# Down products of a two-layer trunk by seven products instead of eight, with the combined down weights summed in DRAM

## The chip, the cores and the metric

The kernel runs on one core of a Trainium2 chip. The metric is the device time of the whole program in microseconds (us), the median of several executions, lower is better. TensorE (PE) multiplies, VectorE (DVE) and ScalarE (ACT) work elementwise, GpSimd (POOL) does small odd jobs, and SyncE (SP) issues the loads. All engines run their own instruction lists and meet at semaphores. Sixteen DMA engines move data between DRAM and the on-chip memory.

## The reference, cut to what matters

512 tokens of width 1024 in float32 go through two layers. In layer 0 the mixer is differential attention beside a gated short convolution, in layer 1 it is a spatial gating unit. Around the mixer and around the feed-forward part stand RMS norms. The feed-forward part of each layer `i`, which the change touches, is

```python
h = rms_norm(x, norm_g[i, 2])
f = (jax.nn.silu(h @ w_gate[i]) * (h @ w_up[i])) @ w_down[i]
x = x + rms_norm(f, norm_g[i, 3])
```

`w_gate` and `w_up` are 1024 x 2816, `w_down` is 2816 x 1024. The last product of that line is called the down product here, and the 512 x 2816 matrix that it takes from the left the hidden matrix.

## The kernel before, in words

**Numbers.** Each float32 operand of a matmul is split into a rounded part `hi` and a rest `lo` (`split`, L136 on ACT and L137 on DVE), and each product is three matmuls: hi by hi, lo by hi, hi by lo (`PASSES`). Splitting 128x1024 elements takes one cast on ACT and one subtraction on DVE.

**Stages.** First come layer 0's projections and attention. Then, in each layer: the output projection of the mixer (`out_proj`), the feed-forward products of gate and up (`ffn`, L550), the down product (`out_proj` again, L110), and the norms between them. Gate and up are computed already by Strassen's scheme: seven products of half-size blocks stand for eight, with combined weights that DVE sums (L215) and combined tokens (`Combined`). The hidden matrix goes to `pair_` tiles, one for each of the 11 units of 256 hidden columns.

**The down product before.** `ffn` ends with `out_proj(Hidden(hidden), 5, ...)`. Eight PSUM banks hold four token tiles by two column halves. For each of the 22 blocks of 128 hidden columns, three matmuls of 128x512 go into each bank: 22 x 8 x 3 = 528 matmuls in each layer. The weights come as 11 chunks of 1 MB and are split in 22 pieces; `Hidden` splits the hidden matrix in 11. The last five blocks are held back, so that the four token tiles end one after the other and `post_norm` of one runs beside the matmuls of the next.

**Order.** `order` and `take` fix the order in which weight chunks are loaded and split, and three `raw` buffers let the loads run ahead. `Clock` counts modelled PE time: `clock.after(wait, step)` writes a step into the program later, `clock.beat` moves the time with each matmul. A scheduler of the framework then lays out each engine's list: among the instructions whose inputs it believes ready it takes the one written first, so an instruction that is written late but has no inputs to wait for can move far ahead on an engine that it believes idle.

**POOL before.** POOL's list is short. In the attention it has one multiplication for each block (`combine`, L732; 4 heads by 4 blocks), whose result DVE adds (L735) and PE transposes (L743), and one power for each norm (`power`, L301). Four pre-norms at the start use the same line. No DMA is issued by POOL; all loads and stores go through SP.

```python
            nc.gpsimd.tensor_scalar(out=probs[1][:, 0:w], in0=probs[1][:, 0:w],
                                    scalar1=c1[:, 0:1], scalar2=None, op0=ALU.mult)
            clock.after(TO_TURN // 2, lambda: turn(at))
```

Of the kernel before, what the change touches and what calls it, by code (L numbers as in the profile page):

```python
# [18 lines left out]
P = 128  # L19
# [6 lines left out]
NF = FFN // P  # L26
RMS_EPS = 1e-6
# [17 lines left out]
class Clock:  # L45
# [4 lines left out]
    def __init__(self):  # L50
        self.now, self.n, self.queue = 0.0, 0, []

# [19 lines left out]
def trunk(  # L72
# [36 lines left out]
    def mm(out, lhsT, rhs, start, stop):  # L109
        nc.tensor.matmul(out, lhsT, rhs, start=start, stop=stop)  # L110
        clock.beat(max(230.0 * rhs.shape[-1] / 512, 108.0))
# [48 lines left out]
    def plan_rows(w, ks):  # L160

        for k in ks[::2]:
            c = Chunk([P, 2, D], [(ALL, w[k * P:(k + 2) * P, :].rearrange("(k p) f -> p k f", p=P))])
            for m in range(2):
                plan(None, c, (ALL, slice(m, m + 1), ALL))

# [61 lines left out]

    FIRST, THEN, STEADY = (7, 3), (1, 2, 4, 6, 5), (1, 2, 4, 6, 5, 7, 3)

    def plan_ffn(layer):
        units = [Unit(layer, c * 256) for c in range(FFN // 256)]
# [10 lines left out]
        plan_rows(w_down[layer], range(NF))  # L243
# [168 lines left out]

    def mean_square(parts):

        ms, a = small(2), small(1)
# [3 lines left out]
        nc.vector.scalar_tensor_tensor(out=a[:, 0:1], in0=ms[:, 0:1], scalar=ms[:, 1:2],  # L419
                                       in1=eps_t, op0=ALU.add, op1=ALU.add)  # L420
        return power(a[:, 0:1], 1), a
# [26 lines left out]
    def post_norm(t, halves, g, wait, then, store):  # L448

        f = row_tile()  # L450
        y0, a = mean_square(halves)
        for n, c in enumerate(HALVES):
            nc.vector.tensor_tensor(out=f[:, c], in0=halves[n], in1=g[:, c], op=ALU.mult)  # L453

        def add():
            y = newton(y0, a[:, 0:1], 1)
            for c in HALVES:
                nc.vector.scalar_tensor_tensor(out=xs[t][:, c], in0=f[:, c], scalar=y,  # L458
                                               in1=xs[t][:, c], op0=ALU.mult, op1=ALU.add)
                if store:  # L460
                    nc.sync.dma_start(out=out[0, t * P:(t + 1) * P, c], in_=xs[t][:, c])
            if then:
                then(t)

        clock.after(wait, add)
# [18 lines left out]
    def out_proj(lhs, n_held, g_post, then, next_ahead, wait=2000, store=False):  # L484
# [13 lines left out]
        for k in range(first):  # L498
            w2 = take(min(2 + k, n_held, n_k - 1 - k))
            lhs.ahead(k + 2)  # L500
# [5 lines left out]
        lhs.ahead(n_k)  # L506
        ahead(n_held)
        held = [take(0) for k in range(n_held)]
        for t in range(NT):
# [3 lines left out]
            post_norm(t, acc[t], g_post, wait, then, store)  # L513
# [3 lines left out]
    class Mixed:  # L517
# [5 lines left out]
        def ahead(self, n):  # L523
            pass

# [3 lines left out]
    class Hidden:  # L529


        def __init__(self, tiles):
            self.tiles, self.n, self.parts = tiles, 2 * len(tiles), []

        def ahead(self, n):
            while 2 * len(self.parts) < min(n, self.n):
                self.parts.append(split(self.tiles[len(self.parts)]))

        def at(self, k, part):
            return self.parts[k // 2][part][:, k % 2, :]  # L540
# [14 lines left out]
    FIRST_TOKENS, LAST_TOKENS = slice(0, 256), slice(256, 512)  # L555

    def ffn(layer, units, hT, g_post, then, next_ahead, store=False):
        hidden = []
# [11 lines left out]
        def finish(c, f, cols, pair_):  # L570

            nc.scalar.activation(out=c[:, 0:256], in_=c[:, 0:256], func=AF.Silu)  # L572
            nc.vector.tensor_tensor(out=pair_[:, f, cols], in0=c[:, 0:256], in1=c[:, 256:512],
# [13 lines left out]
        for i, u in enumerate(units):  # L587
            pair_ = act([P, 2, 512])
            hidden.append(pair_)
# [4 lines left out]
            finish(plus(y, a), 0, LAST_TOKENS, pair_)  # L594
            if i < EARLY:
# [4 lines left out]
                finish(plus(r, u2), 1, LAST_TOKENS, pair_)  # L600
                run(x, u, 5, False)
                v = copied(x)
                finish(plus(z, v), 0, FIRST_TOKENS, pair_)
                finish(plus(x, p7), 1, FIRST_TOKENS, pair_)
# [388 lines left out]
```

## Time and profile before

| what | value |
|---|---|
| median of 3 runs | 1097.82 us (1097.77 to 1098.58) |
| profiled execution, its own time | 1097.55 us |
| its span in the profile | 1095.8 us |
| PE / weight loads / DVE / ACT / POOL busy | 97% / 87% / 66% / 45% / 4% |
| moved by DMA | 111.33 MB, 102 GB/s over the span |

The profile shows one execution. Busy shares are averages over stages that differ; a matmul's own duration overlaps with that of its neighbours, so the pace of PE is read from how many matmuls a stretch of the chain holds. "PEclk" is the clock granted to TensorE as a share of full speed; full speed is the higher of its two levels, 2.4 GHz, and half of it the lower, 1.2 GHz. POOL's instructions stand in the timeline in the order of POOL's list.

### The profile page before, as it was taken

To read this page: it belongs to the slowest core of one execution; us is meant where nothing else is said; L and a number is where in the kernel's file an instruction comes from. 1 tells how busy PE (TensorE), PEld (TensorE's weight loads), DVE (VectorE), ACT (ScalarE), POOL (GpSimd) and SP (SyncE) were. 2 spreads that over 40 slices of the span, in tenths; PEclk is the share of its full clock that TensorE was granted. 3 is DMA by queue.
4 is the path that set the end of the run, shared out by engine and by line. 5 is a ranking of instruction groups with operands and counts; after the bars stand their busy time and mean duration, and the time that the engine had idled before them with its cause. 6 is when DMAs were issued, how large, how long until landed. Compare 5 with 4: busy or idle time off the path is not lost.

```text
span 1095.8 us, 15882 instructions
## 1 busy us (share of the span) xinstructions
PE 1065.2 (97%) x6527; PEld 952.4 (87%) x6527; DVE 728.5 (66%) x1083; ACT 496.8 (45%) x831; POOL 45.2 (4%) x67
## 2 busy tenths in 40 slices
PE   8999999988999999999999999988999999999997
PEld 6777778878999999988888888878999999988886
DVE  4566665598887887873328454779888787883304
ACT  4466444256544454553315333345554454573201
POOL 0011210010000000000001000010000000000000
PEclk8999999998999999999999999998999999999999
DMA  8321222313333233254202231411333323362002
GB/s 314 105 72 59 94 77 79 114 39 118 114 115 116 78 117 116 99 214 149 85 31 78 77 124 69 154 38 59 116 116 108 124 78 115 115 224 87 1 1 77
DMA packets 77770, 111.33 MB, mean 102 GB/s; under 512 B 2769, under 2 KB 63326, under 8 KB 77698
## 3 DMA queue, kind: packets, MB, share of 16 engines
q1 hardware_dynamic: 77698, 110.33, 30.2%
q8 instruction: 51, 0.84, 0.3%
q14 instruction: 21, 0.17, 0.1%
HBM read 108.21 MB, written 2.11 MB: 101 GB/s over the span
## 4 chain that ended last, share of the span: by engine, by line
PE 86%; DVE 8%; ACT 2%; issue 1%; POOL 1%; DMA 1%; SPq 0%; POOLq 0%; DVEq 0%; ACTq 0%
PE ps L110 44%; PE ps L550 38%; DVE wlo L137 1%; DVE hTlo L383 1%; POOL s L301 1%; DVE h L431 1%; ACT j L417 1%; DVE x L458 1%; PE ps L441 1%; PE ps L751 1%; DVE t L388 1%; DMA raw<-in_w_in_even_dram 1%; PE ps L937 1%; DVE wsum L215 1%; ACT whi L136 1%
## 5 line engine op out<-in xcount | busy, mean ns | idle before, releaser
L550 PE MATMUL ps<-hThi,whi 128*128 128x256 f32 x1232 | 276.3, 287 | 7.8 <-ACT hThi L382 7.3
L550 PE MATMUL ps<-hThi,wlo 128*128 128x256 f32 x1232 | 276.7, 285 | 0.0
L550 PE MATMUL ps<-hTlo,whi 128*128 128x256 f32 x1232 | 274.3, 285 | 0.0
L137 DVE TENSOR_TENSOR wlo<-raw,whi 128x1024 fp32r<-128x1024 f32 x166 | 199.0, 1223 | 65.2 <-ACT whi L136 34.4
L550 PEld LDWEIGHTS ps<-hThi,whi 128*128 128x128 f32 x1232 | 205.6, 195 | 10.1 <-ACT hThi L382 8.6
L550 PEld LDWEIGHTS ps<-hThi,wlo 128*128 128x128 f32 x1232 | 206.4, 194 | 0.1
L550 PEld LDWEIGHTS ps<-hTlo,whi 128*128 128x128 f32 x1232 | 204.9, 194 | 0.4 <-DVE hTlo L383 0.4
L136 ACT CAST whi<-raw 128x1024 fp32r<-128x1024 f32 x166 | 169.2, 1047 | 55.0 <-PE ps L110 37.4
L110 PE MATMUL ps<-whi,wlo 128*128 128x512 f32 x352 | 137.1, 390 | 0.0
L110 PE MATMUL ps<-wlo,whi 128*128 128x512 f32 x352 | 137.0, 389 | 0.0
L110 PE MATMUL ps<-whi,whi 128*128 128x512 f32 x352 | 136.7, 389 | 0.0
L137 DVE TENSOR_TENSOR wlo<-wsum,whi 128x1024 fp32r<-128x1024 f32 x88 | 105.8, 1221 | 29.5 <-ACT whi L136 25.7
L136 ACT CAST whi<-wsum 128x1024 fp32r<-128x1024 f32 x88 | 90.1, 1043 | 71.1 <-DVE wsum L215 53.6
L110 PE MATMUL ps<-whi,a 128*128 128x512 f32 x256 | 80.0, 391 | 0.0
L110 PEld LDWEIGHTS ps<-whi,whi 128*128 128x128 f32 x352 | 66.1, 188 | 13.7
L110 PEld LDWEIGHTS ps<-wlo,whi 128*128 128x128 f32 x352 | 66.1, 188 | 13.6
L110 PEld LDWEIGHTS ps<-whi,wlo 128*128 128x128 f32 x352 | 66.1, 188 | 13.5
L572 ACT ACTIVATE t<-t 128x256 f32<-128x256 f32 x88 | 36.1, 417 | 86.0 <-DVE t L562 85.8
L562 DVE TENSOR_TENSOR t<-ps,t 128x512 f32<-128x512 f32 x88 | 58.5, 686 | 15.1 <-PE ps L550 14.4
L567 ACT COPY t<-ps 128x512 f32<-128x512 f32 x70 | 40.8, 583 | 61.2 <-PE ps L550 61.0
L301 POOL TENSOR_TENSOR s<-s,neg_half 128x1 f32<-128x1 f32 (+1 forms) x40 | 25.4, 634 | 960.3 <-DVE s L419 887.2
L453 DVE TENSOR_TENSOR h<-ps,g 128x512 f32<-128x512 f32 x32 | 21.7, 685 | 63.0 <-ACT j L417 63.0
(131 smaller groups left out, 1325.4 us busy)
## 6 DMA issues: line engine op xcount, KB each, us to landing
raw<-in_w_gate_dram SPq DMA_DIRECT2D x44, 512.0 KB, 3.8
raw<-in_w_up_dram SPq DMA_DIRECT2D x44, 512.0 KB, 4.7
raw<-in_w_down_dram SPq DMA_DIRECT2D x22, 1024.0 KB, 4.8
raw<-in_w_in_even_dram SPq DMA_DIRECT2D x10, 1024.0 KB, 5.5
raw<-in_w_in_odd_dram SPq DMA_DIRECT2D x8, 1024.0 KB, 5.1
g<-in_norm_g_dram SPq DMA_DIRECT2D x8, 512.0 KB, 3.7
raw<-in_w_out_even_dram SPq DMA_DIRECT2D x4, 1024.0 KB, 4.8
raw<-in_w_out_odd_dram SPq DMA_DIRECT2D x4, 1024.0 KB, 5.0
```

The source lines that it names most:

```text
L110: nc.tensor.matmul(out, lhsT, rhs, start=start, stop=stop)
L136: nc.scalar.copy(out=hi, in_=src)
L137: nc.vector.tensor_tensor(out=lo, in0=src, in1=hi.bitcast(F32), op=ALU.subtract)
L215: nc.vector.tensor_tensor(out=t, in0=x, in1=y, op=op)
L301: nc.gpsimd.tensor_tensor(out=y0[:, :n], in0=a, in1=neg_half[:, :n], op=ALU.pow)
L383: nc.vector.tensor_tensor(out=lo, in0=src, in1=hi.bitcast(F32), op=ALU.subtract)
L388: minus = lambda out, x, y: nc.vector.tensor_tensor(out=out, in0=x, in1=y, op=ALU.subtract)
L453: nc.vector.tensor_tensor(out=f[:, c], in0=halves[n], in1=g[:, c], op=ALU.mult)
L550: nc.tensor.matmul(bank[:, m * 256:(m + 1) * 256], piece[a][:, m, k, :], hT.at(b, p)[:, k, :], start=first and m == 0 and i == 0, stop=i = ...
L562: nc.vector.tensor_tensor(out=c, in0=x, in1=y, op=ALU.add)
L567: nc.scalar.copy(out=c, in_=x)
L572: nc.scalar.activation(out=c[:, 0:256], in_=c[:, 0:256], func=AF.Silu)
```

## The change

The 2816 rows of the down weights are taken as 11 units of two blocks (j = 0, 1), the 1024 columns as two halves, the 512 tokens as two halves. Seven products of 256 tokens x 1408 x 512 columns replace the eight: 7 products x 11 units x 2 token tiles x 3 = 462 matmuls in each layer. Four of the seven right-hand sides are sums of two, three or four quarters of the down weights.

- `Down.sums` makes these sums in DRAM: four tensors `t` (named `tsum` in the rows) for each layer, each in three groups of 4, 4 and 3 units. A group is copied from one quarter (`ALU.bypass`) and then another quarter or sum is added to it (`ALU.add`), both as DMAs issued by POOL from DRAM to DRAM. That is 24 copies and 24 adds for two layers, up to 1 MB each. `t[2]` needs `t[1]` finished, `t[4]` needs `t[2]` finished.
- These DMAs are handed to `clock.slow`, from which `beat` takes one per 7000 ns of modelled time: layer 0's from the attention on, layer 1's from layer 0's third feed-forward unit on.
- `Down.plan` loads seven quarters or sums per layer through SP, in pieces of at most two units of 512 columns (42 splits for each layer, where there were 22).
- `Hidden` now keeps 12 raw tiles, sums them on DVE in place (`differ`, `piece`: 12 instructions for each layer) and splits 21 pieces (where there were 11).
- `down_proj` runs the products in the order 1, 2, 6, 5, 3, 7, 4 in three pairs of PSUM banks and combines them by ACT copies and DVE additions (`copied`, `plus`). `PostNorm` is the norm after the products with its squares split by column half. The first two token tiles end after the fifth product, the last two after the seventh, of which seven units are held back.
- POOL's space for DMA descriptors grows from 1024 to 4096.

```diff
@@ class Clock
+        self.slow, self.next_slow = [], 0.0
     def beat(self, ns):
         self.now += ns
+        if self.slow and self.now >= self.next_slow:
+            self.next_slow = self.now + 7000
+            self.slow.pop(0)()
@@ trunk
+    class Down:
+        ORDER = (1, 2, 6, 5, 3, 7, 4)
+        GROUPS = (slice(0, 4), slice(4, 8), slice(8, UNITS))
...
+        def sums(self):
+            q, t = self.q, self.t
+            copies = ((t[1], q[0, 0]), (t[3], q[0, 1]), (t[2], q[1, 1]), (t[4], q[1, 0]))
+            adds = ((t[1], q[0, 1]), (t[3], q[1, 1]), (t[2], t[1]), (t[4], t[2]))
+            return [lambda to=to, of=of, g=g, op=op: nc.gpsimd.dma_start(
+                        out=to[:, g, :], in_=of[:, g, :], accum_op=op)
+                    for g in self.GROUPS
+                    for op, pairs in ((ALU.bypass, copies), (ALU.add, adds)) for to, of in pairs]
...
     class Hidden:
+        def differ(self, g):
+            r = self.raw
+            n = act(list(r[0, 0, g].shape))
+            r["n", g] = n
+            nc.vector.tensor_tensor(out=n, in0=r[1, 1, g], in1=r[0, 1, g], op=ALU.subtract)
+            nc.vector.tensor_tensor(out=r[0, 1, g], in0=r[0, 0, g], in1=r[0, 1, g],
+                                    op=ALU.subtract)
...
+    def down_proj(down, lhs, g_post, then, next_ahead, store, wait=2000):
+        n_held = 7
...
+        run(x, 1, last=False)
+        c11 = [copied(x[t]) for t in both]
+        run(y, 2)
...
+        run(x, 6, first=False, last=False)
+        c12 = [copied(x[t]) for t in both]
+        run(q, 5, last=False)
+        c22 = [copied(q[t]) for t in both]
+        run(q, 3, first=False)
+        for t in both:
+            norms[t].close([(1, plus(q[t], c12[t]), -1)])
+        run(x, 7, first=False, last=False)
...
+        finish = run(x, 4, first=False, held=n_held)
+        for t in both:
+            finish(t)
+            norms[t].close([(0, x[t], 1)])
+            ahead(next_ahead[t])
@@ ffn
+            if i == EARLY and layer == 0:
+                clock.slow += downs[1].sums()
...
-        lhs = Hidden(hidden)
-        lhs.ahead(4)
-        out_proj(lhs, 5, g_post, then, next_ahead, store=store)
+        down_proj(downs[layer], hidden, g_post, then, next_ahead, store)
@@ attention
+    clock.slow += downs[0].sums()
     running = [False]
```

How the lists of the engines move is shown at three places. On POOL, from the second pre-norm of the start to the first block of the attention (L301 and L341 are `power`, L732 and L894 the multiplication in `combine`; a wait for DMASW is one for a DMA that POOL issued), before:

```order
L301 TENSOR_TENSOR s_187<-s_181,neg_half 128x1 [waits DVE_49]
L301 TENSOR_TENSOR s_250<-s_244,neg_half 128x1 [waits DVE_49]
L301 TENSOR_TENSOR s_312<-s_306,neg_half 128x1 [waits DVE_49]
L684 MEMSET strip 4x640 [waits PE_49]
L732 TENSOR_SCALAR t_549<-t_549,s_571 128x128 [waits DVE_49,Activation_49]
```

and now, from the same power on (12 rows of which the last is still ahead of the attention):

```order
L341 TENSOR_TENSOR s_195<-s_193,neg_half 128x1 [waits DVE_49]
L191 DMA tsum_81<-in_w_down_dram 128x4x512 [waits DMASW0_49]
L191 DMA tsum_83<-in_w_down_dram 128x4x512 [waits DMASW1_49]
L191 DMA tsum_82<-tsum_81 128x2048 [waits DMASW4_49,DMASW2_49]
L341 TENSOR_TENSOR s_258<-s_256,neg_half 128x1 [waits DVE_49]
L191 DMA tsum_81<-in_w_down_dram 128x4x512
L191 DMA tsum_84<-tsum_82 128x2048 [waits DMASW6_49,DMASW3_49]
L341 TENSOR_TENSOR s_320<-s_318,neg_half 128x1 [waits DVE_49]
L191 DMA tsum_83<-in_w_down_dram 128x4x512
L846 MEMSET strip 4x640 [waits PE_49]
L191 DMA tsum_82<-in_w_down_dram 128x4x512
L191 DMA tsum_84<-in_w_down_dram 128x4x512
```

Four copies stand ahead of these rows, right behind the first power of the program. An add waits on POOL itself until the DMAs whose data it needs have landed, and the powers stand behind it.

On POOL at the end of the attention, the last head, before:

```order
L732 TENSOR_SCALAR t_1334<-t_1334,s_1377 128x128 [waits DVE_49,Activation_49]
L301 TENSOR_TENSOR s_1424<-s_1414,neg_half 128x4 [waits DVE_49]
L732 TENSOR_SCALAR t_1399<-t_1399,s_1453 128x256 [waits DVE_49,Activation_49]
L732 TENSOR_SCALAR t_1483<-t_1483,s_1527 128x384 [waits DVE_49,Activation_49]
L732 TENSOR_SCALAR t_1549<-t_1549,s_1592 128x512 [waits DVE_49,Activation_49]
```

and now:

```order
L894 TENSOR_SCALAR t_1352<-t_1352,s_1396 128x128 [waits DVE_49,Activation_49]
L191 DMA tsum_85<-in_w_down_dram 128x3x512 [waits DMASW7_49]
L191 DMA tsum_87<-in_w_down_dram 128x3x512 [waits DMASW5_49,DMASW1_49]
L191 DMA tsum_86<-tsum_85 128x1536 [waits DMASW4_49,DMASW2_49]
L341 TENSOR_TENSOR s_1443<-s_1433,neg_half 128x4 [waits DVE_49]
L894 TENSOR_SCALAR t_1418<-t_1418,s_1473 128x256 [waits DVE_49,Activation_49]
L191 DMA tsum_88<-tsum_86 128x1536 [waits DMASW6_49,DMASW3_49]
L894 TENSOR_SCALAR t_1503<-t_1503,s_1547 128x384 [waits DVE_49,Activation_49]
L894 TENSOR_SCALAR t_1569<-t_1569,s_1613 128x512 [waits DVE_49,Activation_49]
```

`tsum_85` to `tsum_88` are the sums of layer 1. All 48 DMAs of both layers stand ahead of the multiplications for the last head's third and fourth block; the row `tsum_88<-tsum_86` is the 48th. PE's list of this stage keeps the transposes and projections in nearly the order that they had.

On DVE at the start of layer 0's down product, before (`wlo` are splits, of `raw` weights or of a hidden tile `a`; L562 and L573 end the last feed-forward unit):

```order
L137 TENSOR_TENSOR wlo_4986<-raw_4821,whi_4985 128x1024
L137 TENSOR_TENSOR wlo_5004<-raw_4921,whi_5003 128x1024
L573 TENSOR_TENSOR a_4660<-t_4885 128x256
L137 TENSOR_TENSOR wlo_5008<-a_2766,whi_5007 128x1024
L137 TENSOR_TENSOR wlo_5036<-raw_4921,whi_5035 128x1024
```

and now, during the first product:

```order
L142 TENSOR_TENSOR wlo_5021<-raw_4878,whi_5020 128x1024
L142 TENSOR_TENSOR wlo_5037<-a_2625,whi_5036 128x1024
L614 TENSOR_TENSOR a_5040<-a_2582,a_2516 128x1024
L142 TENSOR_TENSOR wlo_5044<-raw_4878,whi_5043 128x1024
L615 TENSOR_TENSOR a_2516<-a_2620,a_2516 128x1024
L142 TENSOR_TENSOR wlo_5062<-raw_4968,whi_5061 128x1024
```

The sums of `differ` (L614, L615) stand between the splits that the second product takes.

## Rows read from the trace of the kernel before

**Rows 1.** Page: busy time; slices of the span, fortieths from left to right.

```profile
PE 1065.2 (97%) x6527; PEld 952.4 (87%) x6527; DVE 728.5 (66%) x1083; ACT 496.8 (45%) x831; POOL 45.2 (4%) x67
...
PE   8999999988999999999999999988999999999997
...
GB/s 314 105 72 59 94 77 79 114 39 118 114 115 116 78 117 116 99 214 149 85 31 78 77 124 69 154 38 59 116 116 108 124 78 115 115 224 87 1 1 77
```

**Rows 2.** Page: the chain that ended last, shares of the span by engine.

```profile
PE 86%; DVE 8%; ACT 2%; issue 1%; POOL 1%; DMA 1%; SPq 0%; POOLq 0%; DVEq 0%; ACTq 0%
```

**Rows 3.** The chain in order of time: start us, us, what; the down products.

```profile
471.42 105.91 PE ps L110 x467
...
972.93 109.30 PE ps L110 x482
```

**Rows 4.** Stretches: us, busy by engine in order PE, PEld, DVE, ACT, POOL, clock, DMA share, GB/s.

```profile
6.00:154.00 148.00, 141.95 (x671) 110.81 (x670) 89.38 (x219) 78.89 (x185) 19.94 (x22) 0.97 0.33 113
...
6.00:40.00 34.00, 29.57 (x128) 22.60 (x128) 20.21 (x44) 16.70 (x37) 2.22 (x4) 0.85 0.66 241
...
465.00:580.00 115.00, 115.00 (x525) 95.79 (x525) 50.56 (x63) 39.05 (x52) 1.72 (x4) 1.00 0.33 117
```

**Rows 5.** Groups by line, shapes apart: xcount, busy us, mean ns, idle before and its releaser.

```profile
L137 DVE TENSOR_TENSOR wlo<-raw,whi 128x1024 fp32r<-128x1024 f32 x166 | 199.0, 1223 | 65.2 <-ACT whi L136 34.4 <-PE ps L110 26.0 <-issue 3.1
...
L562 DVE TENSOR_TENSOR t<-ps,t 128x512 f32<-128x512 f32 x88 | 58.5, 686 | 15.1 <-PE ps L550 14.4 <-ACT t L567 0.7
L567 ACT COPY t<-ps 128x512 f32<-128x512 f32 x70 | 40.8, 583 | 61.2 <-PE ps L550 61.0
...
L895 DVE SCALAR_TENSOR_TENSOR a<-a,s,g 128x1024 f32<-128x1024 f32 x4 | 5.1, 1285 | 5.5 <-ACT h L893 5.5
```

**Rows 6.** Page: the DMA queue: packets, MB, share of 16 engines' span.

```profile
q1 hardware_dynamic: 77698, 110.33, 30.2%
```

**Rows 7.** DMA issues: KB each, median us from issue to landing.

```profile
raw<-in_w_down_dram SPq DMA_DIRECT2D x22, 1024.0 KB, 4.8
...
out_dram<-x SPq DMA_DIRECT2D x8, 256.0 KB, 2.0
...
x<-in_x_dram SPq DMA_DIRECT2D x2, 256.0 KB, 2.7
```

**Rows 8.** Timeline of POOL: start us, us, line, operation, idle before and its releaser.

```profile
5.28 0.55 POOL L301 TENSOR_TENSOR s<-s,neg_half 128x1 f32<-128x1 f32 x1 [3.76 <-DVE s L419]
16.58 0.55 POOL L301 TENSOR_TENSOR s<-s,neg_half 128x1 f32<-128x1 f32 x1 [10.75 <-DVE s L419]
25.52 0.55 POOL L301 TENSOR_TENSOR s<-s,neg_half 128x1 f32<-128x1 f32 x1 [8.38 <-DVE s L419]
...
60.17 0.61 POOL L732 TENSOR_SCALAR t<-t,s 128x128 f32<-128x128 f32 x1 [26.73 <-DVE s L731]
...
153.94 1.25 POOL L732 TENSOR_SCALAR t<-t,s 128x384 f32<-128x384 f32 x1 [5.50 <-DVE s L731]
160.05 1.57 POOL L732 TENSOR_SCALAR t<-t,s 128x512 f32<-128x512 f32 x1 [4.86 <-DVE t L835]
```

**Rows 9.** Timeline around the first block's multiplication: who takes its result.

```profile
60.82 0.35 DVE L735 SCALAR_TENSOR_TENSOR t<-t,s,t 128x128 f32<-128x128 f32 x1 [0.84 <-POOL t L732]
...
65.90 0.27 PE L743 MATMUL ps<-ident,t 128*128 128x128 f32 x1
```

More of the change, by code (lines that the diff above doesn't have):

```diff
@@ L107, in trunk, with mm @@
     clock = Clock()
[L109 to L110 removed]
+    def mm(out, lhsT, rhs, start, stop, **kw):
+        nc.tensor.matmul(out, lhsT, rhs, start=start, stop=stop, **kw)
         clock.beat(max(230.0 * rhs.shape[-1] / 512, 108.0))
@@ L242, in plan_ffn @@
                 u.plan(p)
-        plan_rows(w_down[layer], range(NF))
+        downs[layer].plan()
         return units
@@ L411, in fill, with root @@
             self.n_turned += 1
+    def root(ms):
+        a = small(1)
+        nc.vector.scalar_tensor_tensor(out=a[:, 0:1], in0=ms[:, 0:1], scalar=ms[:, 1:2],
+                                       in1=eps_t, op0=ALU.add, op1=ALU.add)
+        return power(a[:, 0:1], 1), a
     def mean_square(parts):
-        ms, a = small(2), small(1)
+        ms = small(2)
         for n in range(2):
@@ L512, in out_proj @@
                     products(first + i, t, n, w2)
-            post_norm(t, acc[t], g_post, wait, then, store)
+            PostNorm(t, g_post, wait, then, store).close(
+                [(n, acc[t][n], 1) for n in range(2)])
             if t < 3:
@@ L553, in product, with steps, run, copied @@
                 clock.beat(115.0)
-    FIRST_TOKENS, LAST_TOKENS = slice(0, 256), slice(256, 512)
+    FIRST_TOKENS, LAST_TOKENS = 0, 1
+    def down_proj(down, lhs, g_post, then, next_ahead, store, wait=2000):
+        n_held = 7
+        norms = [PostNorm(t, g_post, wait, then, store) for t in range(2)]
+        x, y, q = ([psum(), psum()] for _ in range(3))
+        def steps(bank, t, units, left, right, first, last):
+            for u in units:
+                for i, (a, b) in enumerate(PASSES):
+                    mm(bank[t], left[u // 4][a][:, u % 4, t * P:(t + 1) * P],
+                       right[u // 2][b][:, u % 2, :], start=first and u == 0 and i == 0,
+                       stop=last and u == UNITS - 1 and i == 2, skip_group_check=True)
+        def run(bank, p, first=True, last=True, held=0):
+            left, right = {}, {}
+            for u0 in range(0, UNITS, 2):
+                units = range(u0, min(u0 + 2, UNITS))
+                if u0 % 4 == 0:
+                    left[u0 // 4] = lhs.take(2 if held and u0 else 1)
+                right[u0 // 2] = take(max(3, held // 2 - u0 // 2) if held else 3, (down, p, u0))
+                if u0 < UNITS - held:
+                    for t in range(2):
+                        steps(bank, t, units, left, right, first, last)
+            rest = range((UNITS - held) // 2 * 2, UNITS) if held else ()
+            return lambda t: steps(bank, t, rest, left, right, first, last)
+        def copied(ps):
+            c = tmp()
+            nc.scalar.copy(out=c, in_=ps)
+            return c
+        def plus(ps, c):
+            nc.vector.tensor_tensor(out=c, in0=ps, in1=c, op=ALU.add)
+            return c
+        both = range(2)
+        run(x, 1, last=False)
+        c11 = [copied(x[t]) for t in both]
+        run(y, 2)
+        for t in both:
+            plus(y[t], c11[t])
+            norms[t].square(0, c11[t])
+            norms[t].scale(0, c11[t], 1)
+        run(x, 6, first=False, last=False)
[6 more added lines that the diff above has]
+        run(x, 7, first=False, last=False)
+        norms = [PostNorm(t, g_post, wait, then, store) for t in range(2, NT)]
+        for t in both:
+            plus(x[t], c22[t])
+            norms[t].square(1, c22[t])
+            norms[t].scale(1, c22[t], -1)
+        finish = run(x, 4, first=False, held=n_held)
+        for t in both:
+            finish(t)
+            norms[t].close([(0, x[t], 1)])
+            ahead(next_ahead[t])
```

137 lines of the change are left out of this document (93 added, 44 removed).

## The prediction

> **What bounds the kernel now.** I read the page first: PE is busy 97% of the span and no other engine over 66% [rows 1]. The chain of waits says the same in another way: 86% of it lies on PE [rows 2]. So a matmul less is time less, wherever PE does not begin to wait for something else. The down products are two unbroken runs in that chain: 467 matmuls in 105.91 us and 482 in 109.30 us [rows 3], 0.2268 us for each. In the first of them DVE is busy 50.56 of 115 us [rows 4], so there is room beside PE. POOL looks free, at 4% of the span [rows 1], but its timeline shows what hangs on it: every block of the attention has one multiplication on POOL, the first at 60.17 us and the last two at 153.94 and 160.05 us, and the pre-norms of the start have a power each [rows 8]. An engine at 4% can still set the end if something long is put ahead of these in its list.
>
> **What the change removes.** 528 matmuls of each down product become 462: 66 fewer in each layer, 132 in all, at 0.2268 us [rows 3]. That is **-29.9 us**, all of it on PE, which sets the end there. The last norm squares one column half late instead of two; under 1 us, left out.
>
> **What it adds in the down products.** DVE first. For each layer there were 33 splits of 128x1024 at 1.223 us [rows 5], 40.4 us. Now there are 63: 49 of that size (59.9 us), 7 of 512 columns at the 0.69 us of an operation of that size and 7 of 768 at some 0.95 us between the two, 71.4 us in all. The sums of `Hidden` add 12 operations: eight of full size at 1.22 to 1.29 us, four of 768, some 14 us. Six additions on PSUM at 0.686 us make 4.1 [rows 5]. So DVE goes from 50.6 us [rows 4] to about 50.6 + 31.0 + 14 + 4.1 = 99.7 us, in a stage that PE now passes in 462 x 0.2268 = 104.8 us. That still fits, at 95%, but the work is uneven: one product takes 15.0 us of PE and its splits 10.2 us of DVE, and the second has the 6.8 us of `differ` between its splits, as the order on DVE shows. Twice in a layer PE also returns to a bank pair that it has just filled and must wait for an ACT copy (0.583 us) or a DVE addition (0.686) [rows 5], which the three matmuls on the other bank (0.68 us) nearly cover. I take 2 us for each layer, **+4 us** in all, between 0 and 13.6 (`differ` wholly exposed in both layers). ACT gains 30 casts a layer of about 1 us or less and stays near two thirds.
>
> The loads grow from 11.5 to 20.2 MB for each layer, 193 GB/s over 104.8 us. The trace has slices of 214 and 224 GB/s with PE at 9 tenths [rows 1]. A chunk of 1 MB lands 4.8 us after its issue [rows 7] and feeds 24 matmuls, 5.4 us, with three buffers. I cost them at nothing; the matmuls are the cover, and without it a chunk would cost its 4.8 us.
>
> **What it adds on POOL.** Here lies the largest term. By the order of POOL, all 48 DMAs that build the sums, those of layer 1 too, stand ahead of the last head's third multiplication, whatever `clock.slow` was meant to space out: the scheduler moved them up. An add waits in POOL's list for the copies that it needs, and everything behind it waits along: the powers of the pre-norms first, then each block of the attention, then DVE's sum and PE's transpose of that block. So the question is when the DMAs are done. Before the multiplication that stood at 153.94 us can run, 24 copies and 23 adds have landed. In pieces of four units (1.05 MB) that is 22 copies and 21.25 adds.
>
> Their price is in no row: the trace before has no transfer from DRAM to DRAM and no adding one. The loads give the scale. Queue 1 moved 110.33 MB in 30.2% of 1095.8 us [rows 6], 333 GB/s while busy, so 1.05 MB takes 3.15 us. A store of 256 KB lands as fast as a load of 256 KB, 2.0 against 2.7 us [rows 7], so writing to DRAM costs about what reading does. A copy does both and lies between 3.15 us (reading hides writing) and 6.3 us (they add up). An add reads two places and writes one: between 3.15 and 9.45 us. I take the middle for the copy, 4.7 us, and half as much again for the add, 7.1 us, three accesses for two; nothing nearer is in the trace.
>
> The Trainium skill, "DMA: Bandwidth & Descriptors", section "Latency and other measured facts", gives 207 to 214 GB/s for copies between DRAM tensors; by it a copy would take 4.9 us, and with an add at half as much again the term below would be 10 us larger; no run here shows it yet.
>
> The sum: the first copy follows the power at 5.28 us, so 5.8. The 22 copies take 103.4 us, the 21.25 adds 150.9. The program's own loads go over the same 16 engines: in the stretch from 6 to 154 us they hold them for 33% of 148 us, 48.8 us [rows 4]. Landing after the transfer, 4.8 - 3.15, is 1.7. Together 310.6 us, where that multiplication stood at 153.94: 156.7 us late. Some of it is spare: the first block's multiplication ended at 60.78, DVE's sum took 0.35 and PE's transpose began at 65.90 [rows 8, 9], 4.8 us. That leaves **+152 us**; with the lower prices it is 34, with the upper 237. PE's own work hides nothing of it, since its list has the transposes in nearly the old places. The waits may take TensorE to its lower clock, as in the start, where the granted clock was 0.85 from 6 to 40 us [rows 4]; PE's 142 us of work in the stretch would even then fit in 284, under the 305 that the DMAs need, so I add nothing.
>
> 1097.55 - 29.9 + 4 + 152 = 1223.6, say **1224 us**, against the profiled execution's own 1097.55, which lies 0.27 under the median shown. The ends: 1097.55 - 29.9 + 0 + 34 = 1102, and with 13.6 and 237, 1318.
>
> **Rivals.**
> *The DMAs keep pace, and the kernel is faster.* Place: POOL's list, the same waits. If copies and adds cost one price p, the delay is 43.25 p + 56.3 - 158.7 (43.25 pieces; start, loads and landing; 153.94 and the 4.8 to spare); it eats the gain of 25.9 us at p = 2.97 us, 353 GB/s. Below that the kernel is faster; at 2.37 us the delay is gone and the time is 1072. For it: POOL's waits of some microseconds ahead of nearly every multiplication [rows 8] leave room to issue. Against it: the loads, which only read DRAM, do not reach 353 GB/s here, and a copy also writes. Chance 0.10.
> *The DMAs run at exactly the loads' price*, 3.15 us for both: 1102 us, or a little less if the program's loads share better than in the sum. Chance 0.07, of which 0.03 lies within 0.2% of no change.
> *An add costs two copies or more.* An add fetches two inputs through the engine that fetches one for a copy; if fetching is what takes the time, an add is 2 x 4.7 = 9.4 us, 21.25 of them 199.8, the delay 201 us and the time 1272. The trace can't tell; the store that lands as fast as a load [rows 7] speaks for neither side being free. Chance 0.25, which holds still slower adds too. The Trainium skill, "Collectives: The Full Stack", section "Part 3: Why 7× under link rate — side-by-side accounting", says that an adding transfer has half the rate of a copy for that very reason; with the 4.9 us above, the time would be 1285. No run here shows it yet.
> *DVE sets the down product.* If all of `differ` is exposed, 13.6 of the 29.9 us go, and the time is 1233; it is inside the range of the forecast and gets no chance of its own.
>
> **How the numbers follow.** The forecast, a POOL list that is late by roughly 80 to 190 us, has the rest, 0.58, with 1150 to 1262 as its own range. Predicted is its middle, 1224. The range of 1100 to 1320 reaches from the loads' price to the upper bounds and leaves out the faster rival and the slowest adds, about 0.2. Two tenths of a per cent, 2.2 us, is about what a measurement of this kernel can tell from no change. Faster: 0.10. Within 0.2%: 0.03. Slower: 0.87.
>
> **What would show it.** In the profile after: the down products as runs of 462 matmuls at 0.227 us, 105 to 109 us long each; POOL's timeline with multiplications that wait long behind DMA issues, the third block of the last head some 150 us later than at 153.94; PE idle in the attention and nowhere else; the share of a new DMA queue near half of the 16 engines until 300 us. A multiplication on POOL at its old time, or 48 DMAs done by about 160 us, would prove the large term wrong. A PE that waits for DVE's splits by more than a few microseconds in the down products would show the small one wrong.

## The result and the profile after

The changed kernel takes **1148.94 us** (median of four), the kernel before 1097.99 us in the same session: a ratio of 1.046, 95% interval 1.044 to 1.048. Three executions lie between 1148.14 and 1149.05 us; the fourth took 1320.78 at a granted clock of 0.74 (the others 0.96) and is left out of the ratio. The kernel is slower by 51 us, where 126 were forecast; the side was right, and the time lies in the range. The execution profiled below took 1149.05 us, span 1147.3.

The page of the changed kernel, busy time, slices of the span, queues (packets, MB, share of 16 engines' span) and the chain by engine:

```profile
PE 1061.2 (92%) x6395; PEld 940.6 (82%) x6395; DVE 812.1 (71%) x1179; ACT 552.9 (48%) x903; POOL 91.9 (8%) x115
...
PE   6796688699889999999999899998899999999997
...
PEclk6798888799989999999999999999999999999999
DMA  9999999953124313423474633241133243245551
...
q1 hardware_dynamic: 83906, 127.63, 33.8%
q0 software_dynamic: 13568, 46.14, 16.1%
...
PE 69%; DMA 15%; DVE 8%; ACT 3%; POOL 3%; issue 2%; SPq 0%; POOLq 0%; DVEq 0%; ACTq 0%
```

Beside [rows 1] and [rows 2]: PE's new holes lie in the first quarter, the deep ones (6 and 7) in the first eight slices, where the row of the DMA engines shows 9s, and the chain has 15% on DMA where it had 1%. Queue 0 is POOL's: 46.14 MB in 16.1% of 1147.3 us, 184.7 us of the engines' time.

POOL's timeline (start us, us, line, operation, idle before and its releaser), pieces from the start to the last head:

```profile
34.75 0.85 POOL L191 DMA_DIRECT2D tsum<-tsum  x1 [13.68 <-DMA tsum<-in_w_down_dram]
35.33 0.87 POOL L341 TENSOR_TENSOR s<-s,neg_half 128x1 f32<-128x1 f32 x1
...
48.17 0.85 POOL L191 DMA_DIRECT2D tsum<-tsum  x1 [11.20 <-DMA tsum<-tsum]
...
93.76 0.85 POOL L894 TENSOR_SCALAR t<-t,s 128x128 f32<-128x128 f32 x1
...
229.52 0.94 POOL L191 DMA_DIRECT2D tsum<-tsum  x1 [6.45 <-DMA tsum<-tsum]
230.19 1.58 POOL L894 TENSOR_SCALAR t<-t,s 128x384 f32<-128x384 f32 x1
237.38 1.56 POOL L894 TENSOR_SCALAR t<-t,s 128x512 f32<-128x512 f32 x1 [5.62 <-DVE t L998]
246.81 1.04 POOL L341 TENSOR_TENSOR s<-s,neg_half 128x4 f32<-128x4 f32 x1 [7.87 <-DVE s L925]
```

The last row is the power after the attention; before, it was

```profile
172.59 1.04 POOL L301 TENSOR_TENSOR s<-s,neg_half 128x4 f32<-128x4 f32 x1 [10.97 <-DVE s L763]
```

POOL's timeline reads as forecast: an add waits for the copy or the sum that it takes, here 6 to 14 us, the powers and multiplications behind it wait along, and the last DMA goes out directly ahead of the last head's third multiplication. That stands at 230.19 us instead of 153.94 [rows 8], 76 us late; the first one already is 33.6 us late (93.76 against 60.17). Loads suffer beside it (DMA issues: KB each, median us to landing). Before:

```profile
raw<-in_w_in_even_dram SPq DMA_DIRECT2D x10, 1024.0 KB, 5.5
...
x<-in_x_dram SPq DMA_DIRECT2D x3, 512.0 KB, 11.1
```

and now:

```profile
raw<-in_w_in_even_dram SPq DMA_DIRECT2D x10, 1024.0 KB, 24.7
...
x<-in_x_dram SPq DMA_DIRECT2D x3, 512.0 KB, 26.1
```

The chain in order of time (start us, us, what) shows both, POOL's waits and a late load, around the first block:

```profile
17.91 16.32 DMA tsum<-in_w_down_dram
34.75 12.84 DMA tsum<-tsum
...
71.03 24.92 DMA raw<-in_w_in_even_dram
```

The first two are the adds at 34.75 and 48.17 us, behind which the powers of the pre-norms stand. The third is a weight load that lands at 95.95 us, while the first block's multiplication (93.76) stands behind an add that has waited for 11.16 us. From there up to the last head's third multiplication, the long pieces of the chain are waits for `tsum`.

A stretch of [rows 4] (busy by engine PE, PEld, DVE, ACT, POOL; clock, DMA share, GB/s), and two of the first down stage:

```profile
6.00:154.00 148.00, 108.77 (x436) 81.10 (x435) 59.19 (x135) 54.58 (x117) 39.84 (x44) 0.83 1.05 292
539.00:615.00 76.00, 76.00 (x350) 63.18 (x349) 71.72 (x74) 50.58 (x64) 0.00 (x0) 1.00 0.64 217
615.00:670.00 55.00, 50.65 (x234) 40.41 (x234) 42.79 (x86) 31.46 (x64) 5.05 (x8) 1.00 0.42 147
```

From 6 to 154 us the DMA engines are full, where they had a share of 0.33. The granted clock of that stretch falls from 0.97 to 0.83, but PE, busy for 108.77 of 148 us, is not what the chain mostly waits for there. And the chain further on, the down products (first and last row) and, between them, a load in the first down stage and the first long run of the next layer:

```profile
545.96 71.32 PE ps L115 x313
...
642.07 5.34 DMA raw<-in_w_in_odd_dram
...
668.29 38.82 PE ps L115 x171
...
1038.53 85.56 PE ps L115 x376
```

Before, the next layer's run was

```profile
601.28 39.91 PE ps L110 x176
```

Where the 51 us come from, by landmarks of both traces: the power after the attention moves from 172.59 to 246.81, +74.2, and the long run of the first down products from 471.42 [rows 3] to 545.96, +74.5, so nothing changes between them. From that run to the first long run of the next layer it takes 122.3 us instead of 129.9, a gain of 7.5; from there to the long run of the second down products (972.93 [rows 3], now 1038.53) 1.4 us are gained, and from that run to the end of the span 14.1. 15 us were forecast for each down stage. Together 74.5 - 7.5 - 1.4 - 14.1 = 51.5, the difference of the spans; the gain behind the attention is 23.0 us.

### The profile page after: what moved, and what is told of

Its sections match the earlier page's. It is cut to its first block, busy times and chain, and to the rows that moved or that the text cites. A ratio compares the mean times of both kernels' runs of the same rounds, so it can differ in the third digit from the quotient of the medians.

```text
span 1147.3 us, 15970 instructions
## 1 busy us (share of the span) xinstructions
PE 1061.2 (92%) x6395; PEld 940.6 (82%) x6395; DVE 812.1 (71%) x1179; ACT 552.9 (48%) x903; POOL 91.9 (8%) x115
## 3 DMA queue, kind: packets, MB, share of 16 engines
q0 software_dynamic: 13568, 46.14, 16.1%
## 4 chain that ended last, share of the span: by engine, by line
PE 69%; DMA 15%; DVE 8%; ACT 3%; POOL 3%; issue 2%; SPq 0%; POOLq 0%; DVEq 0%; ACTq 0%
PE ps L651 37%; PE ps L115 30%; DMA tsum<-in_w_down_dram 7%; DMA tsum<-tsum 4%; DMA raw<-in_w_in_even_dram 3%; DVE wlo L142 1%; POOL s L341 1%; DVE h L475 1%; DVE x L524 1%; ACT j L463 1%; PE ps L485 1%; DVE hTlo L423 1%; POOL tsum L191 1%; PE ps L1100 1%; DVE wsum L254 1%
## 5 line engine op out<-in xcount | busy, mean ns | idle before, releaser
L142 DVE TENSOR_TENSOR wlo<-raw,whi 128x1024 fp32r<-128x1024 f32 (+1 forms) x206 | 239.0, 1183 | 35.7 <-ACT whi L141 35.4
L141 ACT CAST whi<-raw 128x1024 fp32r<-128x1024 f32 (+1 forms) x206 | 203.7, 1018 | 50.4 <-DMA raw<-in_w_in_even_dram 24.2
L115 PE MATMUL ps<-whi,whi 128*128 128x512 f32 x308 | 120.2, 391 | 2.4 <-DVE t L691 2.4
L115 PE MATMUL ps<-whi,wlo 128*128 128x512 f32 x308 | 120.1, 390 | 0.0
L115 PE MATMUL ps<-wlo,whi 128*128 128x512 f32 x308 | 119.9, 389 | 0.0
L341 POOL TENSOR_TENSOR s<-s,neg_half 128x1 f32<-128x1 f32 (+1 forms) x40 | 28.1, 704 | 899.5 <-DVE s L456 842.1
L115 PEld LDWEIGHTS ps<-whi,whi 128*128 128x128 f32 x308 | 57.8, 188 | 15.8 <-issue 3.2
L115 PEld LDWEIGHTS ps<-wlo,whi 128*128 128x128 f32 x308 | 57.8, 188 | 12.0
L115 PEld LDWEIGHTS ps<-whi,wlo 128*128 128x128 f32 x308 | 57.8, 188 | 11.8
L115 PE MATMUL ps<-hThi,wlo 128*128 128x512 f32 x224 | 63.3, 419 | 0.0
## 6 DMA issues: line engine op xcount, KB each, us to landing
raw<-in_w_in_even_dram SPq DMA_DIRECT2D x10, 1024.0 KB, 24.7
```

Source lines behind the costliest of these rows:

```text
L115: nc.tensor.matmul(out, lhsT, rhs, start=start, stop=stop, **kw)
L141: nc.scalar.copy(out=hi, in_=src)
L142: nc.vector.tensor_tensor(out=lo, in0=src, in1=hi.bitcast(F32), op=ALU.subtract)
L341: nc.gpsimd.tensor_tensor(out=y0[:, :n], in0=a, in1=neg_half[:, :n], op=ALU.pow)
```

## Experiments

Ratios are to the kernel before, 95% intervals in brackets.

### 1. Without the sums

```diff
-            src = {1: q[0, 0], 2: q[1, 0], 3: q[1, 1], 4: t[4], 5: t[1], 6: t[2], 7: t[3]}
+            src = {1: q[0, 0], 2: q[1, 0], 3: q[1, 1], 4: q[1, 0], 5: q[0, 0], 6: q[1, 1], 7: q[0, 1]}
-                clock.slow += downs[1].sums()
-    clock.slow += downs[0].sums()
```

> Leaves out the sums in DRAM: no DMA is issued by POOL, and the four summed right-hand sides of the down products are loaded from the quarter that the first copy would have read. Everything else, the 462 matmuls, the splits, the loads and the norms, is as in the change. Theory W (the 48 DMAs ahead of the attention on POOL are the whole loss): the third multiplication of the last head is back near 154 us, 76 us earlier, and the time is about 1149 - 75 = 1074 us, 1070 to 1080. Rival (part of the loss lies in the new down stage itself, its DVE work or its loads): the time stays above 1085 us, and the first down stage is still about 6 us longer than its 462 matmuls.

Measured: 1075.55 us, 0.979 [0.978, 0.981]. POOL's timeline, the first multiplication of the attention and the third of the last head:

```profile
61.48 0.61 POOL L891 TENSOR_SCALAR t<-t,s 128x128 f32<-128x128 f32 x1 [26.75 <-DVE s L890]
...
155.28 1.25 POOL L891 TENSOR_SCALAR t<-t,s 128x384 f32<-128x384 f32 x1 [5.50 <-DVE s L890]
```

So the DMAs cost the change 73 us, and all else in it is a gain of 22. The first down stage is still short of its 15 us: from the start of its long run to that of the next layer it takes 122.2 us (change 122.3, before 129.9). Theory W's number holds, and the rival's small point too: those 7 us do not come from the sums.

### 2. Adds made copies

```diff
-                    for op, pairs in ((ALU.bypass, copies), (ALU.add, adds)) for to, of in pairs]
+                    for op, pairs in ((ALU.bypass, copies), (ALU.bypass, adds)) for to, of in pairs]
```

> Every add becomes a plain copy with the same size, place and wait, so the sums are wrong: what is left out is the adding. Of the 224 us between the first DMA issue and the last on POOL, some 50 are the program's own loads, so 22 copies and 21.25 adds took about 175 us. If an add costs as much as a copy: the last issue stays near 230 us and the time at 1149 us. If it costs one and a half: a copy is 3.25 us, the sums end 34 us earlier, 1115 us. If it costs two: a copy is 2.7 us, the sums end 58 us earlier, 1091 us. The time that queue 0 holds the engines, 184.7 us in the change, says the same a second time.

Measured: 1106.21 us, 1.008 [1.006, 1.009], between the cases of one and a half and two; the last issue is at 183.54 us, 46 us earlier. POOL's queue in this run:

```profile
q0 software_dynamic: 10752, 46.14, 11.5%
```

11.5% of 1105.4 us is 127.1 us for 44 pieces of 1.05 MB, **2.89 us a copy**. In the change 22 copies take 63.6 of the 184.7 us, which leaves 121.1 for 22 adds, **5.5 us an add**: 1.9 copies. This assumes that a copy holds the engines as long in the change as here.

### 3. Nothing behind the DMAs in POOL's list

```diff
-        nc.gpsimd.tensor_tensor(out=y0[:, :n], in0=a, in1=neg_half[:, :n], op=ALU.pow)
+        ln = small(n)
+        nc.scalar.activation(out=ln[:, :n], in_=a, func=AF.Ln)
+        nc.scalar.activation(out=y0[:, :n], in_=ln[:, :n], func=AF.Exp, scale=-0.5)
-        nc.gpsimd.memset(strip, MASKED)
+        nc.vector.memset(strip, MASKED)
-            nc.gpsimd.tensor_scalar(out=probs[1][:, 0:w], in0=probs[1][:, 0:w],
+            nc.vector.tensor_scalar(out=probs[1][:, 0:w], in0=probs[1][:, 0:w],
```

> The 48 DMAs stay where they are at the front of POOL's list, but nothing waits behind them there: the attention's multiplication and the fill of the bias strip go to DVE, and the power of each norm becomes a logarithm and an exponential on ACT (the Newton step after it stays). Theory W (what costs is the wait in POOL's list): the attention is back near its old time, and with some 16 operations more on DVE and some more table loads on ACT the time is 1078 to 1095 us. Rival B (what costs is that the DMAs fill the 16 engines, so that x and the first weights land after 25 us instead of 5 to 11 and the attention starves): the attention still ends 40 us or more late, and the time is above 1115 us.

Measured: 1188.3 us, 1.080 [1.076, 1.084]. The total says little: 80 table loads of 1.28 us on ACT, 103 us, part of them hidden, come from the edit itself. The attention says much. DVE's timeline, the first and the last multiplication:

```profile
94.34 0.29 DVE L896 TENSOR_SCALAR t<-t,s 128x128 f32<-128x128 f32 x1
...
216.09 0.49 DVE L896 TENSOR_SCALAR t<-t,s 128x512 f32<-128x512 f32 x1
```

The first is as late as in the change (93.76) with nothing waiting in POOL's list: late loads can cost these 33 us without it (those of x now land after 32.0 us, and the chain ahead of the first block has a wait of 38.45 us for one of them). It does not follow that in the change the 33 us are late loads. There the chain has the waits of two adds ahead of that block; here the first DMAs start at 1.62 instead of 5.76 us, the loads land later still, and eight of the table loads lie ahead of it. From first to last it is 121.8 us, before 99.9 and in the change 143.6: without waits in the list 22 of the 44 us lost inside the attention remain. That split is rough for the same reasons. With the list free, 56 of the 77 us at the last multiplication remain (216.09 against 160.05). Theory W falls as the only cause.

### 4. The sums of layer 0 alone

```diff
+            if len(downs) > 0 and self is not downs[0]:
+                t = {1: q[0, 0], 2: q[1, 1], 3: q[0, 1], 4: q[1, 0]}
-                clock.slow += downs[1].sums()
```

> The change with the sums of layer 1 left out: 24 DMAs ahead of and in the attention instead of 48, and layer 1's four summed right-hand sides are loaded from plain quarters. Theory A (as forecast: the attention can't end before POOL's list is through, so what counts is when the last DMA is issued): the 24 DMAs are done near 130 to 140 us, before the last blocks, so the attention ends near its old 172 us and the time is 1074 to 1082 us. Theory B (the loads of x and of the first weights are starved while the DMAs run, and PE can't make it up afterwards): the first block is still some 30 us late, as in the change, and stays so; the time is 1100 to 1120 us.

Measured: 1115.64 us, 1.017 [1.015, 1.019], the time of theory B. POOL's timeline:

```profile
91.99 0.86 POOL L894 TENSOR_SCALAR t<-t,s 128x128 f32<-128x128 f32 x1
...
125.03 0.86 POOL L191 DMA_DIRECT2D tsum<-tsum  x1 [6.43 <-DVE wlo L142]
...
192.06 1.25 POOL L894 TENSOR_SCALAR t<-t,s 128x384 f32<-128x384 f32 x1 [5.50 <-DVE s L893]
```

The list is through at 125 us, well ahead of the place where that third multiplication used to stand, and it is still 37 us later than without sums (155.28). 31 of these are there at the first block (91.99 against 61.48), and PE never makes them up: in the kernel before it is busy for 98.38 of the 100 us from 60 to 160. Whether late loads or POOL's list held the first block, this run can't tell; the powers stand behind the adds here too, and the chain has waits of 17.1 and 12.4 us for two adds ahead of it, and one of 22.6 for a weight load across it.

### 5. All DMAs behind the first multiplication

All 48 DMAs behind the first multiplication, kept at their place in program order:

```diff
-    clock.slow += downs[0].sums()
-                clock.slow += downs[1].sums()
+            if (h, qb) == (0, 0):
+                for step in downs[0].sums() + downs[1].sums():
+                    step()
-            return [lambda to=to, of=of, g=g, op=op: nc.gpsimd.dma_start(
-                        out=to[:, g, :], in_=of[:, g, :], accum_op=op)
+            return [lambda to=to, of=of, g=g, op=op: tc.keep_in_program_order(nc.gpsimd.dma_start(
+                        out=to[:, g, :], in_=of[:, g, :], accum_op=op))
```

> The same 48 DMAs, all written right behind the attention's first multiplication and kept in program order: none ahead of the first block, so x and the first weights land as before and the first multiplication is at 60 us; but now seven or eight of them stand ahead of each of the next seven multiplications, and the last before the ninth block. If only starved loads count, what the change loses ahead of the first block (33 us) is saved and the rest stays: 1105 to 1120 us. If the place in POOL's list counts as forecast, the ninth multiplication waits for all 48: 60 + 185 us of DMAs + some 30 of loads = 275 us where it stood near 113, the eight blocks behind it need some 45 us more, and the time is about 1075 + 150 = 1225 us, 1190 to 1250.

Measured: 1240.79 us, 1.130 [1.128, 1.132], inside what the place in the list was to give. POOL's timeline, then two stretches:

```profile
61.22 0.62 POOL L892 TENSOR_SCALAR t<-t,s 128x128 f32<-128x128 f32 x1 [26.75 <-DVE s L891]
61.78 3.23 POOL L191 DMA_DIRECT2D tsum<-in_w_down_dram  x4
...
274.39 0.87 POOL L191 DMA_DIRECT2D tsum<-tsum  x1 [8.21 <-issue]
275.02 1.86 POOL L892 TENSOR_SCALAR t<-t,s 128x512 f32<-128x512 f32 x1
```

```profile
60.00:150.00 90.00, 35.53 (x140) 26.97 (x138) 19.01 (x40) 20.00 (x38) 23.27 (x25) 0.68 0.96 245
150.00:270.00 120.00, 24.51 (x94) 19.14 (x95) 13.94 (x39) 12.50 (x35) 28.39 (x30) 0.59 0.95 226
```

The last DMA goes out at 274.39 us (expected 275), directly ahead of the eighth block's multiplication (the ninth was expected), and PE works 24.5 of the 120 us from 150 to 270. The chain between holds waits for `tsum`, POOL's own instructions and idle time without a releaser in the profile, but no load of the program: here the place in the list is what costs. The same 48 DMAs cost 73 us where the scheduler had put them, and 165 here (1240.79 - 1075.55).

### 6. Pinned, but not paced

The DMAs kept at their written place, and nothing else:

```diff
-            return [lambda to=to, of=of, g=g, op=op: nc.gpsimd.dma_start(
+            return [lambda to=to, of=of, g=g, op=op: tc.keep_in_program_order(nc.gpsimd.dma_start(
```

> The same 48 DMAs, each kept at its place in program order, so that POOL issues one for every 7 us of modelled time: layer 0's beside the attention, layer 1's beside layer 0's feed-forward part. Theory W: a DMA needs 4.2 us of the engines on average, less than the 7 us step, so no wait on POOL grows, and the time is 1075 to 1095 us. Rival B (the traffic itself slows loads wherever it stands): the attention or the feed-forward part of layer 0 loses what the traffic takes, some 90 us of engine time for each layer, and the time stays above 1120 us.

Measured: 1099.13 us, 1.001 [1.000, 1.002], between both. The power after the attention is back at 172.10 us, as theory W wants. But the long run of the first down product starts at 494.33 us, 21 us later than without sums (473.14). POOL's timeline and a stretch of the feed-forward part:

```profile
259.89 0.81 POOL L191 DMA_DIRECT2D tsum<-tsum  x1 [6.15 <-issue]
260.42 3.33 POOL L191 DMA_DIRECT2D tsum<-in_w_down_dram  x4
```

```profile
300.00:360.00 60.00, 53.71 (x429) 53.31 (x428) 43.33 (x50) 26.22 (x37) 11.87 (x14) 0.94 1.06 303
```

and a piece of the chain in that stretch:

```profile
313.93 19.48 DMA raw<-in_w_up_dram
```

The place in program order paces nothing there: POOL has next to no other work in the feed-forward part, so it issues four DMAs at once as soon as an add lets it, the engines are full again, and the chain waits for weights: without sums (experiment 1) PE is busy for all 60 us of that stretch. No instruction that the stage needs stands behind these DMAs, so here late loads cost without any wait in the list.

### 7. Spread by data

```diff
+        if clock.slow and clock.now >= clock.next_slow:
+            clock.next_slow = clock.now + clock.step
+            i = (slice(None),) + (0,) * (len(shape) - 2) + (slice(0, 1),)
+            tc.keep_in_program_order(nc.gpsimd.tensor_scalar(
+                out=small(1)[:, 0:1], in0=lo.bitcast(F32)[i], scalar1=neg_half[:, 0:1],
+                scalar2=None, op0=ALU.mult))
+            clock.slow.pop(0)()
         return hi, lo
...
     ffn(0, units0, hT, g_post, next_layer, (3, 6))
+    clock.slow += downs[1].sums()
```

The step is 13000; the like lines in `beat` and in `ffn` go, and the DMAs are pinned.

> All 48 DMAs stay, each tied to a weight split: a tiny POOL operation reads one column of the split that DVE has just written, and the DMA stands behind it, one for every 13 us of modelled time, layer 0's from the attention on, layer 1's from the start of layer 1 on. Theory B (what costs is that DMAs in a bunch fill the 16 engines and starve the loads): a copy and an add hold the engines for 2.9 and 5.5 us, under half of each step, so nothing is starved; the attention ends near 172 us, the feed-forward part of layer 0 loses nothing, and the time is near that without sums, 1075 to 1082 us. Rival (the traffic costs time wherever it stands, since loads and sums share DRAM): 185 us of engine time more, of which a tenth or more shows, 1092 us or above, like the run in which POOL's list was only pinned (1099 us).

Measured: **1077.6 us, 0.982 [0.980, 0.983]**. Theory B's time. POOL's timeline at a step in the feed-forward part:

```profile
270.74 1.11 POOL L143 TENSOR_SCALAR s<-wlo,neg_half 128x1 f32<-128x1 f32 x1 [16.77 <-DVE wlo L139]
271.80 0.77 POOL L195 DMA_DIRECT2D tsum<-in_w_down_dram  x1
```

POOL now waits 16.8 us for a split and then issues one DMA. All 185 us of traffic (196 in this run) are still there and cost 2 us against the run without sums, whose interval touches this one. Against experiment 6 three things changed: the tie to data, the step (13 instead of 7 us) and the start of layer 1's sums. Which of them a smaller edit could leave out was not tested; that traffic beside the feed-forward part as such costs little is shown, since 200 us of it (270 to 470) have PE busy for 199.8. This version, which computes what the reference does, beats both kernels.

### 8. Spread, and the norms of the first two token tiles later

```diff
-        norms = [PostNorm(t, g_post, wait, then, store) for t in range(2)]
+        norms = [PostNorm(t, g_post, 12000, then, store) for t in range(2)]
```

> As the spread DMAs, and one number more: the norms of the first two token tiles follow 12 us instead of 2 us of modelled time after their product, so that DVE's list has the splits for the seventh product ahead of the chain of small norm steps. Theory (the 6 to 7 us that the first down stage lost are DVE waiting inside that chain while PE needs splits): 5 to 8 us faster than the spread DMAs alone, 1068 to 1075 us. Rival (PE waits there for loads, with no split ready whatever DVE does): within 2 us of the spread DMAs alone.

What this edit is after is DVE's list in the change, here behind the end of product 3:

```profile
617.30 1.37 DVE L691 TENSOR_TENSOR t<-ps,t 128x512 f32<-128x512 f32 x2 [2.70 <-PE ps L115]
...
620.44 0.16 DVE L347 TENSOR_TENSOR s<-s 128x1 f32<-128x1 f32 x1 [0.30 <-POOL s L341]
...
623.40 0.22 DVE L456 SCALAR_TENSOR_TENSOR s<-s,eps_t 128x1 f32<-128x1 f32 x1 [0.96 <-ACT j L463]
...
638.12 0.47 PE L115 MATMUL ps<-whi,whi 128*128 128x512 f32 x1 [2.25 <-DVE t L691]
```

Small steps of two norms wait for ACT and POOL in turn, with no split between them, and PE has only 50.65 busy of the 55 us from 615 on. The last row is PE's longest idle time there: it ends not with a split but with the addition (L691) that frees the bank of product 7, to which DVE comes late. Measured with the edit: 1075.61 us, 0.980 [0.979, 0.982], the fastest that computes what the reference does; 2.0 us less than experiment 7, which lies at the rival's bound, so the theory's 5 to 8 us did not come. The trace shows what it did. Two stretches, around the seventh product and behind it, first in experiment 7, then in this one:

```profile
550.00:570.00 20.00, 17.03 (x82) 13.32 (x81) 17.43 (x35) 13.00 (x27) 1.10 (x2) 1.00 0.17 52
570.00:600.00 30.00, 28.61 (x132) 22.95 (x131) 22.92 (x45) 16.88 (x33) 3.75 (x6) 1.00 0.64 216
```

```profile
550.00:570.00 20.00, 19.45 (x94) 16.08 (x93) 13.70 (x33) 6.75 (x20) 1.10 (x2) 1.00 0.16 52
570.00:600.00 30.00, 28.01 (x130) 22.45 (x129) 23.48 (x47) 19.27 (x38) 4.65 (x6) 1.00 0.55 182
```

PE's idle time falls from 2.97 to 0.55 us in the first stretch and grows from 1.39 to 1.99 in the second. The stage is 3.3 us shorter (119.0 instead of 122.3 us). The chain of this stage still holds a wait for the next layer's first mixer weights, 5.04 us here, 5.28 in experiment 7 and 5.34 in the change, so the rival, loads, is not ruled out for the rest; what is left of the 15 was not pursued.

## Why the prediction was right in its sign and wrong in its size

**The matmuls, -29.9 us.** Right at its base: 313 matmuls in 71.32 us and 376 in 85.56 are 0.228 us each, against 0.227 in [rows 3]. 23.0 us of it arrived, 22 by experiment 1.

**DVE in the down products, +4 us, 0 to 13.6.** About 7 us (29.9 - 23.0), inside the bounds, but only partly at a place named. `differ` cost nothing in layer 0: PE works 76 of 76 us in the stretch from 539 to 615, with DVE at 71.7, 94%, close to the 95% forecast. In that stretch the loads cost nothing either, as costed: 217 GB/s with PE full. The loss lies behind product 3. PE's return to a bank, which the working counts as nearly covered, is 2.25 us of the 4.35 that PE idles there. DVE comes late to it behind the norm chain in its list, of which the working does not speak (experiment 8 took 3.3 us off the stage by moving that chain); how much of the rest is the weight load in the chain stays open.

**The failed step: the term of +152 us for POOL's list.** Its prices were too high, 4.7 us for a copy and 7.1 for an add; experiment 2 gives 2.89 and 5.5. The working priced a copy between "reading hides writing" and "they add up", and took the middle; for the copy the lower end was nearest, and even that (3.15 us) a little high; the add lies near the middle of its bounds, 3.15 to 9.45. The same sum with measured prices: 5.8 + 22 x 2.89 + 21.25 x 5.5 + 48.8 + 1.7 = 236.8 us, less 153.94 and the 4.8 to spare, **78 us**. The trace shows 74.2 behind the attention. With 78 in place of 152, and the +4 as taken, the forecast would have been 1150. Since the add's price is itself read from the change's trace, this shows that the sum holds together, not that it was confirmed a second time.

**The mechanism was half of it.** Experiment 5 shows that a place in POOL's list costs about what the forecast says. But the sum looks only at where the last DMA stands. It lets the program's loads simply take their 48.8 us and puts no price on their lateness, and it lets the attention make up whatever was lost ahead of that DMA. With half the DMAs the same formula gives 5.8 + 11 x 2.89 + 11 x 5.5 + 48.8 + 1.7 = 148.6 us, no delay at all; experiment 4 measured 37 us at that multiplication. In the change both causes end at about the same time, since both are the same work through the same 16 engines, so the formula came near with the right prices. Of the 77 us at the last multiplication (237.38 against 160.05), 33 lie ahead of the first block and 44 in the attention. Without waits in the list 56 of the 77 remained in experiment 3, some of them its own table loads, and the sum, which prices the list alone, gives 78: the two overlap, and how the 77 divide in the change itself is not shown.

**The rivals.** An add does cost about two copies: 1.9. The Trainium skill, "Collectives: The Full Stack", section "Part 3: Why 7× under link rate — side-by-side accounting", says of the adding step of a collective that it runs at half the rate of a copy because it reads two sources. The ratio agrees with experiment 2; the reason no run here shows. The time of that rival, 1272, did not come, because the copy was not 4.7 us. The 207 to 214 GB/s that the Trainium skill gives for copies between DRAM tensors ("DMA: Bandwidth & Descriptors", section "Latency and other measured facts") stand there for copies issued from the sync and scalar queues, with other row pitches. POOL's copies in experiment 2 reach more: 1.05 MB in 2.89 us of the engines is 363 GB/s. "The DMAs keep pace" had its break-even at one price of 2.97 us for both; experiment 2 has that price (2.89), and is 8.5 us slower than before, not level. Its last DMA goes out at 183.54 us, within 2.2 us of the formula's 181.3; but the attention ends 31.3 us late (its last power at 203.90 against 172.59) where the formula, less the 4.8 to spare, has 22.6, and the gain behind it is 21.7 instead of 25.9. The 4.8 us to spare did not show.

**What was to show it.** Matmuls at 0.228 us, the multiplications behind DMA issues and PE's idle time in the attention came as named. The runs were broken, 313 and 376 matmuls instead of 462. The third block was to be 150 us late (76), queue 0 near half of the engines until 300 us; it held 184.7 of the first 235, and then nothing. PE idled in the first down stage too, where the text had it idle in the attention and nowhere else.

## What to carry to other kernels

DMAs that had nothing to wait for were moved ahead to wherever the scheduler found their engine idle; to pace such a DMA, give it data to wait for, such as a tiny operation on the same engine that reads what the main work has just written. Look at background traffic from two sides: as a wait for all that stands behind it in its queue, and as lateness of every load that runs beside it, the first loads of the program above all. The two overlap, so they do not add up, and time lost early is not made up where PE is full. The same 48 DMAs took the kernel from 1149 us to 1099 when pinned, to 1078 when paced by data, and to 1241 at a worse place.

## What the runs showed of the hardware

- A copy from DRAM to DRAM held the 16 engines for 2.89 us per 1.05 MB, less than the 3.15 us of a load by [rows 6]; an adding one for 5.5 us (experiment 2). Spaced out, as in experiment 7, four single copies landed 5.1 to 7.2 us after their issue.
- POOL itself spends about 0.8 us on issuing a 1 MB copy, 1.3 us on adding a piece of the weights and 0.9 us on adding another sum (0.77, 1.32 and 0.87 us at 271.80, 284.07 and 321.96 us of experiment 7).
- With both queues full, POOL's queue took most of the engines' time, 78% of the first 235 us of the change against 23% for the loads, and a 1 MB load landed after a median of 24.7 us instead of 5.5.
- TensorE's granted clock was 0.59 of full speed, between its two levels and nearer the lower (1.2 GHz), over 120 us of experiment 5 in which PE was busy for 24.5, and 0.97 over the next 60 us, with PE busy for 56.8.
